# One side's products of the inverse joins as 32 of 32x64 instead of 64 of 32x32

## The chip, the cores and the metric

The kernel runs on one core of a Trainium2 chip. The metric is the device time of one execution in microseconds; the time of a version is the median of several runs. The engines are named as in the profile: PE is TensorE (PEld its weight loads), DVE is VectorE, ACT is ScalarE, POOL is GpSimd and SP is SyncE.

## The reference, cut to what matters

One layer of a hybrid encoder on 528 tokens (16 meta tokens and 512 of the input), model width 1024. Beside an attention branch and an MLP it has a recurrent branch with 8 heads of width 64, a delta rule that goes token by token:

```python
def step(S, inp):
    rt, wt, kt, vt, at, bt = inp
    sa = jnp.einsum('bhij,bhj->bhi', S, at)
    S = S * wt[:, :, None, :] + sa[..., None] * bt[:, :, None, :] + vt[..., None] * kt[:, :, None, :]
    yt = jnp.einsum('bhij,bhj->bhi', S, rt)
    return S, yt

_, y = lax.scan(step, s0, xs)
```

The two branches are gated, projected and added to the residual; then comes an MLP with a squared ReLU of inner width 4096. Everything is float32.

## The kernel before

The recurrence is done in 9 chunks of 64 tokens. Within a chunk the delta rule needs the inverse of a unit triangular 64x64 matrix, one for each head and chunk. The function `inverse` (line 960) makes them for a group of four heads at a time; there are two groups, so it runs twice, g = 0 and g = 1. Four heads lie as two pairs (`pr_`), two heads of a pair on the two halves of the 128 partitions.

An inverse is made from small blocks upwards. DVE inverts the 16x16 diagonal blocks by 15 steps of substitution (lines 985 and 986), all blocks at once. Then come two joins on PE. In the first, 16x16 blocks are joined to 32x32 ones; each of the four quadrants of 32 partitions (`qs[0]` to `qs[3]`) holds one such block. In the second (lines 1033 and 1040), the even and the odd quadrant of a head are joined to the 64x64 inverse. The first join has three groups of products for the 16 cells (8 chunks by 2 pairs):

- line 1011: the lower blocks times `Dn`, the inverses of the 16x16 blocks; DVE masks the result into `W2` (line 1012; the trace calls this tile AX, whose memory it has);
- line 1017: the inverse times `W2`, which line 1021 adds to `Dn`. `Dn` is then read by line 1033, and only its quadrants 0 and 2;
- line 1020: `W2` times the inverse, which line 1025 adds to `Tt`, the placed inverse. `Tt` is read by lines 1040 and 1099.

`Tt` has 64 columns for each cell: in an even quadrant the 32x32 inverse stands in columns 0 to 31 and zeros in columns 32 to 63, in an odd quadrant the other way round (line 993).

The products are in float32, so that PE makes each of them in two passes: 64 products are 128 MATMUL instructions in the trace, and 128 LDWEIGHTS (weight load) instructions on PEld beside them.

All of the first half of the kernel is emitted by a planner, the classes `Clock` and `Turns` (lines 63 and 150). The recurrent branch, the attention, its features and the projections of the input (`projections`, line 553, its matmuls in line 579) are generators that emit some instructions and then give a time from which they can go on. The planner emits the one with the best rank that is ready at its own modelled PE time, and fills with projections (rank 8) otherwise. That order is PE's program order, fixed at build time. The modelled cost of a matmul (lines 121 to 131) hangs on its columns and its tile, with 0.1 us when the tile's form changes; thus an edit of a few matmuls can move the order of those behind it. PE executes strictly in that order. DVE and ACT follow the order too, within the scheduler's priorities.

Behind an inverse stands the chain of its group (`chain`, line 1044): for each of 9 chunks line 1093 on PE, `Rs` on DVE, line 1099 on PE, `uv` on DVE, line 1121 on PE, the next state on DVE. Projections and attention are laid between them. In the second half of the kernel (from line 1222), output projections and MLP, PE goes through matmul after matmul.

Of the kernel before, what the change touches and what calls it, by code (L numbers as in the profile page):

```python
# [187 lines left out]
def kernel(ctx, tc, ht, x, win, par, cst, gain, lora, wout, wo, wup, wdn, out, dbg=None):  # L188
    nc = tc.nc
    dbg = dbg or {}  # L190
    mm = nc.tensor.matmul
# [94 lines left out]
    with ExitStack() as st:  # L286
# [213 lines left out]
        Tt = rp.tile([128, NCH, 2, 64], F32, name="Tt")  # L500
# [4 lines left out]
        hss = [slice(0, 64), slice(64, 128)]  # L505
# [454 lines left out]
        def inverse(g, Bms, late):  # L960
# [35 lines left out]
            Dn, W2 = (AX_[i][:, :64 * LIVE].rearrange("p (a b) -> p a b", b=32) for i in (1, 0))  # L996
            V.tensor_copy(Dn, At[:, :, 2:n2].rearrange("p t n -> p n t"))
            qs = [slice(32 * q, 32 * q + 32) for q in range(4)]
            cells = [(2 * c + pr_ - 2, pr_, c) for c in range(1, NCH) for pr_ in range(2)]

            def half(q):
                return qs[q % 2]

            def bank(name):
                return psm(name).rearrange("p (a b) -> p a b", b=32)

            yield lambda: max(ck.ready(Dn), banks(1))
            p1 = bank("pw")
# [4 lines left out]
            yield lambda: max(ck.ready(W2, Tt), banks(2))  # L1013
            p1, p2 = bank("pw"), bank("pw")
            for n, pr_, c in cells:
                for q in range(4):
                    mm(p1[qs[q], n, :], Tt[qs[q], c, pr_, half(q)], W2[qs[q], n, :], start=True, stop=True)
            for n, pr_, c in cells:
                for q in range(4):
                    mm(p2[qs[q], n, :], W2[qs[q], n, :], Tt[qs[q], c, pr_, half(q)], start=True, stop=True)  # L1020
# [9 lines left out]
            p1 = bank("pw")  # L1030
# [6 lines left out]
            p1 = bank("pw2")  # L1037
# [133 lines left out]
        def recurrent():  # L1171
# [4 lines left out]
            for g in range(2):  # L1176
                prs = pairs[2 * g:2 * g + 2]
                for j, q in enumerate(prs):
# [19 lines left out]
                    if j == 0 and g > 0:  # L1198
                        yield normalised[0][1]
                    yield from q.bonus()  # L1200
                yield from inverse(g, [q.Bm for q in prs], (lambda: pairs[2].ask_keys(inverted[0])) if g == 0 else lambda: None)
                inverted[g].done = True
                turns.add(0, chain(g, prs))
# [30 lines left out]
    with ExitStack() as st:  # L1234
# [5 lines left out]
        for m in range(KB):  # L1240
            w = ahead.pop() if ahead else load_w(wout[m])
            pp = []
            for br in range(2):
# [4 lines left out]
                n = 0  # L1248
# [59 lines left out]
        for i in range(4):  # L1308
            po = ppo()
            n = 0  # L1310
# [289 lines left out]
```

## Time and profile before

| | |
|---|---|
| time, median of 3 runs | 837.0 us (835.97 to 838.46) |
| time of the profiled execution | 836.0 us |
| its span in the profile | 834.2 us |
| PE busy | 810.9 us, 97% |
| DVE busy | 605.0 us, 73% |
| ACT busy | 452.7 us, 54% |
| mean granted clock of PE | 0.994 |
| first inverse, lines 1011 to 1040 | 112.9 to 131.8 us |
| second inverse, lines 1011 to 1040 | 285.4 to 305.9 us |

A row of the timeline reads: start in us from the span's start, duration in us, engine, line, operation, tile written and tiles read, tile of the array (rows*columns), operand shape, how many instructions were put together, and in brackets the engine's idle time before them with what ended it. "issue" there means that nothing in the profile ended it. Matmuls are pipelined, so the rows of consecutive groups overlap. A row of the windows has the busy time and, in brackets, the number of instructions of each engine in that stretch, then the granted clock of PE (1.00 is full speed) and the DMA load. A row of the waits has the total in us, the number of times and the longest. The rows of the DMA queues have packets, MB, and the time of the packets as a share of 16 engines' time.

### The profile page before, as it was taken

The page shows a single profiled execution, that of the slowest core. Times are in us where ns is not written, and L with a number is a line of the kernel's source. Part 1 is how long each engine was busy: PE and PEld are TensorE (multiplying, and loading weights), DVE is VectorE, ACT ScalarE, POOL GpSimd, SP SyncE. Part 2 cuts the span into 40 slices and gives each one's busy share as a digit, 9 for nine tenths or more (in the row PEclk, how much of TensorE's full clock was granted, in tenths as well). Part 3 has the DMA queues.
Part 4 walks back from the last instruction along what each step waited for, and adds up shares of the span by engine and source line. Part 5 has one row for each costly group of instructions (what it writes and reads, how often), then busy time and mean ns, then how long its engine had stood idle before and what let it go on. Part 6 is the DMA issues. An engine that isn't in the chain of part 4 may idle for free.

```text
span 834.2 us, 15768 instructions
## 1 busy us (share of the span) xinstructions
PE 810.9 (97%) x6014; PEld 666.4 (80%) x6014; DVE 605.0 (73%) x1197; ACT 452.7 (54%) x941; POOL 123.1 (15%) x123
## 2 busy tenths in 40 slices
PE   8989989999999899999999999999999999999998
PEld 6979877777868777677878889888888888888886
DVE  6797975596878836676356744975698679867988
ACT  7767537766666347764456623665345434543452
POOL 1031000010001000000022002100650074007400
PEclk9999999999999989999999999999999999999999
DMA  7231221221121402123587603632743274336532
GB/s 239 69 100 55 74 70 55 65 83 59 51 90 52 128 28 79 43 85 102 171 274 223 214 14 122 182 102 59 244 155 98 90 226 153 87 113 203 157 109 75
DMA packets 51484, 95.90 MB, mean 115 GB/s; under 512 B 5832, under 2 KB 7240, under 8 KB 51408
## 3 DMA queue, kind: packets, MB, share of 16 engines
q1 hardware_dynamic: 47680, 86.37, 32.8%
q0 software_dynamic: 1280, 4.20, 1.7%
q10 hardware_dynamic: 2448, 4.33, 1.5%
q8 instruction: 47, 0.77, 0.4%
q14 instruction: 29, 0.24, 0.1%
HBM read 88.56 MB, written 6.31 MB: 114 GB/s over the span
## 4 chain that ended last, share of the span: by engine, by line
PE 85%; DVE 7%; ACT 3%; issue 2%; DMA 2%; SPq 0%; DVEq 0%; ACTq 0%
PE pj L579 22%; PE po L1341 21%; PE po L1468 12%; PE pd L1468 5%; PE po L1251 4%; PE po L1313 3%; PE pj L394 1%; PE pd L1282 1%; PE po L1282 1%; PE psc L740 1%; PE py L794 1%; PE psr L948 1%; PE pssq L674 1%; DVE wlo L549 1%; PE ppt L777 1%
## 5 line engine op out<-in xcount | busy, mean ns | idle before, releaser
L579 PE MATMUL pj<-uhi,whi 128*128 128x264 f32 (+1 forms) x480 | 166.8, 347 | 0.0
L579 PE MATMUL pj<-uhi,wlo 128*128 128x264 f32 (+1 forms) x480 | 154.5, 322 | 2.5 <-DVE wlo L549 2.5
L579 PE MATMUL pj<-ulo,whi 128*128 128x264 f32 (+1 forms) x480 | 154.5, 322 | 0.0
L240 DVE TENSOR_TENSOR wlo<-wraw,whi 128x512 fp32r<-128x512 f32 x84 | 82.5, 993 | 33.5 <-ACT whi L240 33.5
L579 PEld LDWEIGHTS pj<-uhi,whi 128*128 128x128 f32 x480 | 91.0, 190 | 13.7 <-issue 5.3
L579 PEld LDWEIGHTS pj<-uhi,wlo 128*128 128x128 f32 x480 | 90.9, 189 | 9.8 <-DVE wlo L549 2.9
L579 PEld LDWEIGHTS pj<-ulo,whi 128*128 128x128 f32 x480 | 91.2, 190 | 6.6 <-issue 1.9
L1341 PE MATMUL po<-zlo,whi 128*128 128x512 f32 (+1 forms) x248 | 94.8, 382 | 0.0
L1341 PE MATMUL po<-zhi,whi 128*128 128x512 f32 (+1 forms) x248 | 94.8, 382 | 0.0
L1341 PE MATMUL po<-zhi,wlo 128*128 128x512 f32 (+1 forms) x248 | 94.8, 382 | 0.0
L240 ACT CAST whi<-wraw 128x512 fp32r<-128x512 f32 x84 | 51.2, 616 | 51.4 <-PE po L1341 17.0
L548 ACT CAST whi<-wraw 128x512 fp32r<-128x512 f32 x78 | 47.8, 617 | 43.4 <-PE pj L579 40.7
L549 DVE TENSOR_TENSOR wlo<-wraw,whi 128x512 fp32r<-128x512 f32 x78 | 53.8, 695 | 17.6 <-ACT whi L548 17.2
L1390 POOL TENSOR_TENSOR t<-traw 128x512 f32<-128x512 f32 x24 | 38.6, 1626 | 173.1 <-DMA traw<-in_wdn 120.9
L274 ACT CAST whi<-t 128x512 fp32r<-128x512 f32 x64 | 39.9, 623 | 44.5 <-DVE wlo L274 27.2
L1468 PE MATMUL po<-wlo,fhi 128*128 128x512 f32 (+1 forms) x164 | 63.4, 387 | 0.1
L1468 PE MATMUL po<-whi,flo 128*128 128x512 f32 (+1 forms) x164 | 62.8, 384 | 0.0
L1468 PE MATMUL po<-whi,fhi 128*128 128x512 f32 (+1 forms) x164 | 62.3, 384 | 0.0
L274 DVE TENSOR_TENSOR wlo<-t,whi 128x512 fp32r<-128x512 f32 x64 | 43.5, 689 | 24.3 <-ACT whi L274 24.0
L1357 ACT CAST fhi<-R 128x768 fp32r<-128x768 f32 (+1 forms) x32 | 30.2, 944 | 48.3 <-DVE R L1364 24.9
L1341 PEld LDWEIGHTS po<-zhi,wlo 128*128 128x128 f32 x248 | 46.6, 188 | 9.1
L1341 PEld LDWEIGHTS po<-zlo,whi 128*128 128x128 f32 x248 | 46.6, 188 | 9.1
(330 smaller groups left out, 1701.8 us busy)
## 6 DMA issues: line engine op xcount, KB each, us to landing
wraw<-in_win SPq DMA_DIRECT2D x84, 256.0 KB, 2.6
wraw<-in_wup SPq DMA_DIRECT2D x60, 256.0 KB, 3.1
wraw<-in_wdn SPq DMA_DIRECT2D x48, 256.0 KB, 2.7
traw<-in_wdn SPq DMA_DIRECT2D x48, 256.0 KB, 3.5
gd<-gt ACTq DMA_DIRECT2D x16, 256.0 KB, 2.2
wraw<-in_wout SPq DMA_DIRECT2D x16, 256.0 KB, 3.8
gl<-gd SPq DMA_DIRECT2D x16, 256.0 KB, 3.5
traw<-in_wdn POOLq DMA_DIRECT2D x16, 256.0 KB, 3.1
```

The source lines that it names most:

```text
L240: casts.append((A.copy(hi, raw), low.tensor_tensor(lo, raw, hi.bitcast(F32), ALU.subtract)))
L274: return A.copy(hi, x), V.tensor_tensor(lo, x, hi.bitcast(F32), ALU.subtract)
L548: after(A.copy(hi, raw), last["ACT"])
L549: after(V.tensor_tensor(lo, raw, hi.bitcast(F32), ALU.subtract), last["DVE"])
L579: mm(po, a, b[:, k, a0:a1], start=n == 0, stop=n == 23)
L1251: mm(po, a, ys[k][:, b, :], start=n == 0, stop=n == 11)
L1282: mm(pd[i], a[:, k, 128 * i:128 * i + 128], b, start=k == 0 and n == 0, stop=k == 7 and n == 2)
L1313: mm(po, a[:, k, 128 * i:128 * i + 128], b[:, k, :], start=n == 0, stop=n == 23)
L1341: mm(po[:, t0:t1], a, b[:, k, t0:t1], start=n == 0, stop=n == 23)
L1357: A.copy(fhi[:, j, a:b], R[:, a:b])
L1390: eng.tensor_tensor(t, sums[c, pair] if c in (T1, T2) else c, d, ALU.add)
L1468: mm(x[i][:, cols], a[:, k, left, 128 * rows:128 * rows + 128], c[:, cols], start=start and k == 0 and n == 0, stop=stop and k == n_pairs ...
```

## The change

```diff
             for n, pr_, c in cells:
-                for q in range(4):
-                    mm(p1[qs[q], n, :], Tt[qs[q], c, pr_, half(q)], W2[qs[q], n, :], start=True, stop=True)
+                for e, hs in enumerate(hss):
+                    mm(p1[hs, n, :], Tt[qs[2 * e], c, pr_, :], W2[qs[2 * e], n, :], start=True, stop=True)
```

For each cell line 1017 now makes two products in place of four. Each takes an even quadrant's rows of `Tt` with all 64 columns as weights and the same quadrant of `W2` as the moving operand, 32 columns, and writes 64 partitions: an even quadrant gets what it got, the odd one beside it gets zeros, since there `Tt` has its zeros. The update of the odd quadrants of `Dn` is left out with that; no later line reads them. Line 1020 and all else stay as written.

The planner's order changes with it. PE in the first inverse, as a difference; the name behind the arrow's first comma is the weights (`Tt`), the one before it the moving operand (AX is `W2`):

```order
 L579 MATMUL pj<-ulo,whi 128x512
 L579 MATMUL pj<-uhi,wlo 128x512
-L1017 MATMUL pw<-AX_1271,Tt 32x32 x64
+L1017 MATMUL pw<-AX_1271,Tt 64x32 x32
 L1020 MATMUL pw<-Tt,AX_1271 32x32 x64
 L579 MATMUL pj<-uhi,whi 128x512
```

Only line 1017's group has changed there: 32 products, 64 MATMUL and 64 LDWEIGHTS instructions in place of 128 and 128. Up to the second inverse PE has no other row in a new place.

PE in the second inverse, as a difference (pj are the projections):

```order
-L1017 MATMUL pw<-AX_3662,Tt 32x32 x64
-L1020 MATMUL pw<-Tt,AX_3662 32x32 x64
+L1017 MATMUL pw<-AX_3630,Tt 64x32 x32
+L1020 MATMUL pw<-Tt,AX_3630 32x32 x64
+L579 MATMUL pj<-uhi,whi 128x512
+L579 MATMUL pj<-ulo,whi 128x512
+L579 MATMUL pj<-uhi,wlo 128x512
 L579 MATMUL pj<-uhi,whi 128x512
 L579 MATMUL pj<-ulo,whi 128x512
```

Three projection matmuls have moved ahead of the attention's scores (line 740) that follow, and line 1033 stands after nine projections and these scores, where it stood after twelve. Line 1040 follows nine projections behind line 1033, as before; the three that are left over come behind line 1040.

PE at the second chain's first step, before (pch and Rs are the chain's tiles, ppt the attention's transposes):

```order
L1093 MATMUL pch<-uv,L_3467 64x64
L775 MATMUL ppt<-cs,pm_450 48x128
L777 MATMUL ppt<-cs,pe_4121 128x128 x2
L777 MATMUL ppt<-cs,pe_4129 128x128 x2
L1099 MATMUL pch<-Rs,Tt 64x64 x4
```

and now:

```order
L1093 MATMUL pch<-uv,L_3435 64x64
L579 MATMUL pj<-uhi,whi 128x264
L579 MATMUL pj<-ulo,whi 128x264
L579 MATMUL pj<-uhi,wlo 128x264
L579 MATMUL pj<-uhi,whi 128x264
L579 MATMUL pj<-ulo,whi 128x264
L579 MATMUL pj<-uhi,wlo 128x264
L1099 MATMUL pch<-Rs,Tt 64x64 x4
```

Between lines 1093 and 1099 six short projections stand where the transposes stood. Such shifts go on through the first steps of the second chain; from its fifth chunk on the order is that of before again.

## The prediction

> **What bounds the kernel now.** I read the page first.
>
> ```profile
> span 834.2 us, 15768 instructions
> PE 810.9 (97%) x6014; PEld 666.4 (80%) x6014; DVE 605.0 (73%) x1197; ACT 452.7 (54%) x941; POOL 123.1 (15%) x123
> q8 instruction: 47, 0.77, 0.4%
> PE 85%; DVE 7%; ACT 3%; issue 2%; DMA 2%; SPq 0%; DVEq 0%; ACTq 0%
> ```
>
> PE is busy 97% of the span and is 85% of the chain that ended last. What PE saves or loses reaches the end nearly whole, unless a later wait takes it back. So the next view is what PE waits for, its two longest entries, and those of line 1011 and of the chain:
>
> ```profile
> PE pw L1020 <- issue: 5.8, 2, 3.5
> PE pj L579 <- DVE wlo L549: 2.5, 1, 2.5
> ...
> PE pw L1011 <- DVE AX L997: 1.8, 2, 0.9
> PE pch L1099 <- DVE Rs L1095: 1.7, 3, 0.7
> ```
>
> The largest wait of the whole execution stands in line 1020, right behind the edited products: 5.8 us in two holes, and nothing in the profile ends them. The timeline of PE around the first inverse, then the second:
>
> ```profile
> 117.22 1.26 PE L1017 MATMUL pw<-AX,Tt 32*32 32x32 f32 x126
> ...
> 118.33 1.07 PE L1020 MATMUL pw<-Tt,AX 32*32 32x32 f32 x102
> 121.72 0.46 PE L1020 MATMUL pw<-Tt,AX 32*32 32x32 f32 x24 [2.32 <-issue]
> 122.10 0.80 PE L579 MATMUL pj<-uhi,whi 128*128 128x512 f32 x1
> ...
> 126.53 1.20 PE L1033 MATMUL pw<-AX,Bm 32*32 32x32 f32 x64
> 127.66 0.73 PE L740 MATMUL psc<-ka,qa 64*128 64x272 f32 x4
> 128.32 0.50 PE L579 MATMUL pj<-uhi,whi 128*128 128x512 f32 x1
> ...
> 130.59 1.20 PE L1040 MATMUL pw<-Tt,W 32*32 32x32 f32 x64
> ```
>
> ```profile
> 286.55 0.50 PE L579 MATMUL pj<-uhi,whi 128*128 128x512 f32 x1
> ...
> 288.79 1.26 PE L1017 MATMUL pw<-AX,Tt 32*32 32x32 f32 x126
> ...
> 293.88 1.50 PE L1020 MATMUL pw<-Tt,AX 32*32 32x32 f32 x95 [3.52 <-issue]
> ...
> 300.94 1.20 PE L1033 MATMUL pw<-AX,Bm 32*32 32x32 f32 x64
> ```
>
> Line 1020 stops in its middle, where no instruction has anything to wait for: 102 of its passes are through in the first case, about 33 in the second. The windows show that each hole costs twice, since the granted clock falls to half behind it (0.50 in the column behind POOL):
>
> ```profile
> 118.49:121.90 3.41, 1.09 (x125) 0.97 (x116) 1.49 (x3) 0.54 (x2) 0.00 (x0) 1.00 0.04 12
> 121.90:125.31 3.41, 3.41 (x32) 2.67 (x21) 1.41 (x2) 0.00 (x0) 0.00 (x0) 0.50 0.02 5
> ...
> 292.57:295.98 3.41, 2.10 (x97) 1.94 (x97) 0.54 (x1) 0.00 (x0) 0.00 (x0) 0.50 0.02 5
> 295.98:299.39 3.41, 3.41 (x10) 1.86 (x9) 2.06 (x8) 0.31 (x1) 0.00 (x0) 0.50 0.00 0
> ```
>
> **Where the holes come from.** My reading is that PE has run out of program. The page's q8 is a queue of 47 packets, kind "instruction", 0.77 MB. PE and PEld have 12,028 instructions; 0.77 MB over these is 64 bytes each, and 12,028 / 47 is 256 in a packet. So q8 carries PE's program, 256 instructions at a time. The windows from the start to each hole count what had been issued:
>
> ```profile
> 0.00:120.50 120.50, 112.81 (x1240) 97.98 (x1241) 97.54 (x211) 78.66 (x163) 15.71 (x37) 1.00 0.33 105
> 0.00:292.50 292.50, 276.39 (x3017) 230.19 (x3018) 224.94 (x553) 183.64 (x423) 24.68 (x51) 0.99 0.27 85
> ```
>
> That is 2,481 and 6,035, and their difference, 3,554, is 14 packets of 256 less 30 (semaphore events of PE's queue are not in these counts). So both holes stand at a packet's edge. And packets come in just there. In the DMA queues asked by window, 118.9 to 120.3 has the first of these rows, 120.4 to 121.7 none; 286.6 to 287.9 has the second, 287.9 to 291.5 none, 291.5 to 292.5 the third:
>
> ```profile
> q8 instruction: 1, 0.02, 5.7%
> ```
>
> ```profile
> q8 instruction: 1, 0.02, 5.3%
> ```
>
> ```profile
> q8 instruction: 1, 0.02, 5.5%
> ```
>
> In both cases PE goes on soon after a packet that began late. A packet spans 17.7 us on average (834.2 / 47); lines 1017 and 1020 with 512 instructions burn two in 2.3 us. How fast can packets follow each other? PE passed the edge before the first hole at instruction 2,481 - 256, which is 203 instructions into line 1017, at 118.1; the next packet could be used at 121.72, 3.6 us later. In the second, from 289.05 (61 into line 1017) to 293.88, 4.8 us. So 256 instructions need 3.6 to 4.8 us of supply, and the holes are that less the 1.1 us in which PE used them.
>
> **The change part by part.**
>
> *The 32 products themselves.* They are 64 passes instead of 128. Before, four quadrants ran side by side, 128 passes in 1.1 us. Lines 1033 and 1040 are 64 passes of the same 32 moving columns on two quadrants, and take 1.20 as rows, 1.1 to the next group: half the products, the same time, since each quadrant still makes 32 passes. The new line 1017 also has two row groups, so it gains nothing on PE itself. It may lose, because its weights have 64 columns. The nearest rows for that:
>
> ```profile
> L1033 PEld LDWEIGHTS pw<-AX,Bm x128: 101/108/109, 126.5 to 301.9; 32*32 32x32 f32 x128
> ```
>
> ```profile
> L1099 PEld LDWEIGHTS pch<-Rs,Tt x144: 129/134/136, 139.1 to 375.5; 64*64 64x64 f32 x144
> ```
>
> 32 more weight columns make a load 26 to 28 ns longer. A pass in a quadrant now takes 1.1 us / 32 = 34 ns; if the load hides behind the pass, line 1017 stays at 1.1 us; if it sets the pace, a pass is about 34 + 26 = 60 ns, and line 1017 takes 1.9 us. I take 1.85 (+0.75 each time), since the load is now twice as wide as the operand that would have to hide it; both ends stay for the range. A gain is excluded: per row group the passes are the same 32.
>
> *Two changes of the array's form* in place of none, between the new tile (32x64) and line 1020's: bounded by nothing below and a matmul's whole length above (about 0.2 us, each L1033 pass); I take 0.1 per inverse.
>
> *128 instructions less in each inverse.* This is the term that counts, because the edges of the packets stay where they are in the count and the program slides past them. First inverse: the edge of the hole was instruction 459 from line 1017's start (256 + 203). Lines 1017 and 1020 are now 128 + 256 = 384 long, so it lies 75 behind them: past the twelve projections (24 instructions), 51 into line 1033. From the edge before it (75 into line 1020) PE now takes 181 / 256 of 1.1 us, 0.1, the twelve projections, and 51 / 128 of line 1033. Nine projections took 130.59 - 128.32 = 2.27 us at full clock, twelve are 3.03. Sum 0.78 + 0.1 + 3.03 + 0.45 = 4.4 us against a supply of 3.6 to 4.8: a hole of 0 to 0.4.
>
> Second inverse: its edge was 317 behind line 1017's start, which itself now comes 128 earlier: 445, or 61 past line 1020's end, 35 into line 1033 (9 projections and the scores are 26). From the edge before, 61 into line 1020: 0.84 + 0.1 + 2.27 + 0.66 (scores, 128.32 - 127.66) + 0.31 = 4.2 us, a hole of 0 to 0.6. And the edge before that now lies at the end of line 1011: 0.2 + 2.24 (286.55 to 288.79) + 1.1 to 1.85 + 0.26 = 3.8 to 4.5 us, a hole of 0 to 1.0. I take 0.3 for each inverse. Holes this short are below the 2.3 and 3.5 us that cost clock, so the half-speed stretches go too.
>
> On this the Trainium skill speaks against me: "Runtime: NRT & Kernel Launch", section "Instruction fetch mechanics", has the program fetched in blocks of 256 instructions while the engine executes, and calls that cost mostly hidden, because dispatch is slower than the fills. The block agrees with 12,028 / 47; that dispatch is slower does not hold in line 1017's row. By its rule the holes are something else and stay, and the sum below would be rival 2's.
>
> *What the waits behind it do.* Line 1033 needs line 1025 on DVE:
>
> ```profile
> 122.22 1.41 DVE L1025 SCALAR_TENSOR_TENSOR Tt<-pw,even,Tt 128x512 f32<-128x512 f32 x2 [2.00 <-PE pw L1020]
> ```
>
> 1.41 us, under the nine to twelve projections (2.27 to 3.03 us) between lines 1020 and 1033; without them PE would wait these 1.4. DVE now has line 1021 ahead of one softmax step in each inverse, so that this step waits for line 1017's end; it sits idle there anyway (2.00 above). The moved rows of the second inverse and the chain are the same work in another place, taken at nothing; they hide behind projections, and the price if they don't is rival 4.
>
> **The sum**, against the profiled execution. First inverse, from line 1017's start to line 1033's: 126.53 - 117.22 = 9.31 us before; 1.85 + 0.1 + 1.1 + 3.03 = 6.08 now: 3.2 us less. Second: 300.94 - 288.79 = 12.15 before; the same pieces (twelve projections, the scores) 6.08 + 0.66 = 6.74 now: 5.4 us less. Together 8.6, less 0.6 for short holes: 8.0 us. The profiled execution took 836.0 us, so 828.0; it was 1.0 below the median of 837.0, and the forecast for the median is 829.0. With weights hidden and no hole left the gain is 10.7 (about 826.5); with the short holes at their long end it is 8.6 - 2.0 = 6.6 (830.5).
>
> **The rivals.**
>
> 1. *Part of it comes back.* Either the lead of the first inverse is eaten before the second, where DVE's steps (lines 985 to 997) decide when line 1011 can start, and only 5.4 - 0.3 = 5.1 us stay (832); or the short holes come at their long end, 2.0 us, with one half-speed window of 3.41 us, worth 1.7, left: 8.6 - 3.7 = 4.9 us, also 832. For it: line 1011 waited for DVE before (1.8 us in two). Against: behind the first hole DVE sat idle, so it moves forward with PE. Chance 0.25.
>
> 2. *The holes are no code loading* and come again behind line 1017 at full length, with the half clock. Then only the weight loads tell: 0 to 2 x 0.75 us more, 837.0 to 838.5. The packet edges speak against. Chance 0.09. The page of the skill named above stands on this side.
>
> 3. *The diff does nothing*, because line 1017 is no shorter in time: 837.0, as in 2 and counted there. The order shows 32 for 64, so the instructions do go.
>
> 4. *Slower: the second chain's new order.* With lines 1093, 1099 and 1121 elsewhere among the projections, PE reaches a step before DVE has its operand and stands, strictly in order. Before, the longest such wait was 0.7 us (line 1099 in the waits). If each of the 9 chunks waited 1.2 us more, that is 10.8 against the 8.0 gained: 839.8. It decides from 0.9 us in each chunk. Against it: six projections still stand between lines 1093 and 1099. Chance 0.06.
>
> **How the numbers follow.** The forecast has 0.60, rival 1 0.25, rivals 2 and 3 0.09, rival 4 0.06. A measurement here tells about 0.3% (2.5 us) from no change. The forecast and rival 1 are faster by more: 0.85, of which I give 0.01 to "same" for rival 1 falling short: 0.84; same 0.10; slower 0.06. For the range, the forecast's own ends are 826.5 and 830.5; half a microsecond of scatter below, and rival 1 with the runs' scatter of 1.5 above, give 826.0 to 833.5.
>
> **What would show it.** Right: no "issue" wait of over 1 us in line 1020, PEclk at full speed in both inverses, line 1017 with 64 passes in 1.1 to 1.9 us, line 1033 about 3 and then 8 us earlier than before. Short holes, if any, in line 1033. Wrong: the holes still in line 1020; or gone while PE's waits for DVE grow by as much.

## The result and the profile after

The changed kernel takes 828.63 us, the median of 4 runs (827.75 to 828.87). The kernel before, on the same chip, took 837.15 (835.97 to 838.46, 4 runs). The ratio is 0.9896, with a 95% interval of 0.9879 to 0.9913. The forecast was 829.0 in a range of 826.0 to 833.5. The profiled execution took 828.85 us, where that of before took 836.0; their spans are 7.1 us apart. The last experiment below had one run of 996.73 us at a mean granted clock of 0.751, which its figure leaves out.

The page of the changed kernel, its lines on the span, the engines, the program queue and the chain:

```profile
span 827.1 us, 15510 instructions
PE 809.1 (98%) x5886; PEld 666.0 (81%) x5886; DVE 603.5 (73%) x1197; ACT 452.7 (55%) x941; POOL 123.4 (15%) x123
q8 instruction: 46, 0.75, 0.4%
PE 84%; DVE 9%; ACT 4%; issue 2%; DMA 1%; DVEq 0%; ACTq 0%; SPq 0%
```

PE has 128 MATMUL and 128 LDWEIGHTS instructions fewer, and q8 brings one packet fewer: 11,772 / 46 is again 256 in a packet. PE's busy time fell by only 1.8 us. Its idle time, the span less the busy time, fell by 5.3 us, from 23.3 to 18.0. The longest wait of PE after the change, and two that the prediction speaks of:

```profile
PE pj L579 <- DVE wlo L549: 2.5, 1, 2.5
...
PE pw L1011 <- DVE AX L997: 1.8, 2, 0.9
...
PE pch L1099 <- DVE Rs L1095: 1.4, 2, 0.8
```

Line 1020, which led this list with 5.8 us, is no longer in it, and line 1033 has not come in. The wait of line 1099 is 1.4 us, where it was 1.7. The timeline of PE around the first inverse:

```profile
118.67 2.05 PE L1017 MATMUL pw<-AX,Tt 32*64 32x32 f32 x64
...
120.65 1.29 PE L1020 MATMUL pw<-Tt,AX 32*32 32x32 f32 x128
121.87 0.50 PE L579 MATMUL pj<-uhi,whi 128*128 128x512 f32 x1
...
124.81 1.20 PE L1033 MATMUL pw<-AX,Bm 32*32 32x32 f32 x64
```

and around the second:

```profile
287.04 2.05 PE L1017 MATMUL pw<-AX,Tt 32*64 32x32 f32 x64
...
289.02 1.29 PE L1020 MATMUL pw<-Tt,AX 32*32 32x32 f32 x128
290.24 0.50 PE L579 MATMUL pj<-uhi,whi 128*128 128x512 f32 x1
...
293.38 1.20 PE L1033 MATMUL pw<-AX,Bm 32*32 32x32 f32 x64
...
298.25 0.50 PE L579 MATMUL pj<-uhi,whi 128*128 128x512 f32 x1
```

Line 1020 now runs through, 128 passes in one row with no bracket. The windows over the same stretches (line 1017's start to line 1033's) show PE busy throughout at full clock, 1.00 in the column behind POOL, where there were half-speed windows before:

```profile
118.67:124.81 6.14, 6.14 (x205) 5.29 (x204) 3.66 (x11) 2.43 (x9) 0.00 (x0) 1.00 0.15 47
287.04:293.38 6.34, 6.34 (x207) 4.95 (x206) 4.52 (x17) 1.52 (x6) 0.00 (x0) 1.00 0.27 90
```

The edited products themselves got slower. Line 1017 takes 118.67 to 120.65, that is 1.98 us, where it took 1.1. Its view by source line shows why (the times are shortest, median and longest in ns):

```profile
L1017 PEld LDWEIGHTS pw<-AX,Tt x128: 128/133/133, 118.7 to 288.8; 32*64 32x64 f32 x128
L1017 PE MATMUL pw<-AX,Tt x128: 217/218/239, 118.7 to 288.9; 32*64 32x32 f32 x128
```

A weight load of 64 columns takes 133 ns, against 108 for 32 columns in line 1033. The two row groups each make 32 passes in 1.98 us, the step to line 1020 included; that is 62 ns a pass, where it was 34.

One stretch differs by accident, ahead of the inverses. In each profiled execution PE waits 2.5 to 2.8 us for DVE (the first row of the waits above), here from 49.0 to 51.5 us, and in this one the clock fell to half behind it for 3.41 us. The windows for the same stretch, before and after the change:

```profile
51.50:57.00 5.50, 5.50 (x66) 4.04 (x67) 5.47 (x10) 1.77 (x5) 2.37 (x3) 1.00 0.56 181
```

```profile
51.50:57.00 5.50, 5.50 (x39) 4.07 (x40) 4.89 (x9) 0.97 (x4) 2.37 (x3) 0.69 0.62 186
```

Half of 3.41 us is 1.7. So line 1011 starts at 114.4 after the change and at 112.9 before, though PE's program is the same up to there. From line 1011's start to the end it is 827.1 - 114.4 = 712.7 us after, and 834.2 - 112.9 = 721.3 before: 8.6 us less. The experiments below are compared by this stretch too, since what is placed or lost ahead of it is not in it.

### The profile page after: what moved, and what is told of

Same layout as the page of the kernel before. It is cut to its first block, busy times and chain, and to the rows that moved or that the text cites. A ratio compares the mean times of both kernels' runs of the same rounds, so it can differ in the third digit from the quotient of the medians.

```text
span 827.1 us, 15510 instructions
## 1 busy us (share of the span) xinstructions
PE 809.1 (98%) x5886; PEld 666.0 (81%) x5886; DVE 603.5 (73%) x1197; ACT 452.7 (55%) x941; POOL 123.4 (15%) x123
## 4 chain that ended last, share of the span: by engine, by line
PE 84%; DVE 9%; ACT 4%; issue 2%; DMA 1%; DVEq 0%; ACTq 0%; SPq 0%
PE po L1341 21%; PE pj L579 21%; PE po L1468 12%; PE pd L1468 5%; PE po L1251 4%; PE po L1313 3%; PE pj L394 1%; PE po L1282 1%; PE pd L1282 1%; PE psr L948 1%; PE psc L740 1%; PE py L794 1%; DVE wlo L549 1%; PE pssq L674 1%; PE ppt L777 1%
## 5 line engine op out<-in xcount | busy, mean ns | idle before, releaser
L240 DVE TENSOR_TENSOR wlo<-wraw,whi 128x512 fp32r<-128x512 f32 x84 | 77.6, 934 | 35.2 <-ACT whi L240 35.1
L549 DVE TENSOR_TENSOR wlo<-wraw,whi 128x512 fp32r<-128x512 f32 x78 | 53.7, 695 | 18.7 <-ACT whi L548 18.3
L1341 PEld LDWEIGHTS po<-zhi,whi 128*128 128x128 f32 x248 | 46.6, 188 | 9.0
```

The costliest lines, as they stand in the source:

```text
L240: casts.append((A.copy(hi, raw), low.tensor_tensor(lo, raw, hi.bitcast(F32), ALU.subtract)))
L549: after(V.tensor_tensor(lo, raw, hi.bitcast(F32), ALU.subtract), last["DVE"])
L1341: mm(po[:, t0:t1], a, b[:, k, t0:t1], start=n == 0, stop=n == 23)
```

## The experiments

**Theory.** PE runs out of program at a packet's edge when two packets are used up faster than one arrives. The change wins because 128 instructions fewer in each inverse put the edges where PE uses its program slowly; the products themselves lose. **Rival A:** the holes belong to lines 1017 and 1020, to their tiles or their waits, and the new form of line 1017 removes them. **Rival B** (by the rule of the Trainium skill, "Runtime: NRT & Kernel Launch", section "Instruction fetch mechanics", that the loading of program is mostly hidden): the holes are no code loading at all, and would not follow a count of instructions.

Three kinds of edit tell them apart: unused products added 100 us ahead, which shift the edges and touch nothing else; a pause between lines 1017 and 1020, which thins the burst and leaves all products; and the products of the even quadrants alone in the old form, which save the same number of instructions as the change. The line numbers of the rows are shifted where an edit adds lines above: with 18 or 32 unused products, lines 579, 1017 and 1020 of the kernel are 581, 1019 and 1022, with the pause line 1020 is 1022, and with two adds for line 1021 line 1033 is 1034. The kernel before was run again beside the experiments, 13 times each: 837.41 us beside the first four, 836.37 beside the last four. The ratios are to these.

### 72 unused instructions ahead, in the changed kernel

```diff
                     mm(warm[:, :128], ones, ones, start=True, stop=True)
+                for i in range(18):
+                    mm(warm[:32, :32], ones[:32, :32], ones[:32, :32], start=True, stop=True)
```

> The changed kernel with 18 extra 32x32 products (72 instructions of PE) in the warm-up at the start, where PE stands waiting anyway; the rest of PE's order is the same. Theory (PE's program comes in packets of 256, and a packet that PE uses up in less than 3.6 to 4.8 us leaves a hole): the edges of the packets move 72 instructions earlier in the program, so that nearly a whole packet is line 1020's burst (1.2 to 1.3 us). A hole of 2.3 to 3.6 us comes back in both inverses, right behind the end of line 1020 in the first and some ten instructions before its end in the second, each with half clock behind it; 8 to 10 us slower than the changed kernel, 834 to 840 us, although the inverses are untouched. Rival (fewer products in line 1017 are what helped, or the holes belonged to the tile of line 1017): no hole, 828 to 830 us.

Measured: 834.99 us (830.95 to 841.98, 10 runs), ratio to before 0.9984 (0.9955 to 1.0013); the profiled execution took 833.74. That is 6.4 us above the changed kernel, and the two intervals of the ratio do not meet. The timeline of PE in the two inverses:

```profile
123.57 0.40 PE L581 MATMUL pj<-uhi,whi 128*128 128x512 f32 x1
124.23 0.39 PE L581 MATMUL pj<-ulo,whi 128*128 128x512 f32 x1 [0.27 <-issue]
...
290.42 1.25 PE L1022 MATMUL pw<-Tt,AX 32*32 32x32 f32 x125
...
293.49 0.31 PE L1022 MATMUL pw<-Tt,AX 32*32 32x32 f32 x3 [1.81 <-issue]
```

The windows from the start into each hole:

```profile
0.00:123.90 123.90, 117.26 (x1240) 101.70 (x1241) 98.70 (x213) 78.74 (x163) 15.68 (x37) 0.99 0.33 102
0.00:293.00 293.00, 279.66 (x3017) 233.25 (x3018) 225.22 (x553) 183.75 (x423) 24.66 (x51) 0.99 0.27 85
```

1240 + 1241 is 2,481 and 3017 + 3018 is 6,035: the holes have come back at the very instruction numbers they had before the change. In the first inverse that number now falls among the projections behind line 1020, and not into its products. This is against both rivals. The sizes were missed: 0.3 and 1.8 us where 2.3 to 3.6 was expected, and 6.4 us of loss where 8 to 10 was. In the first hole 256 instructions lie between 121.59 and 124.23, so this packet was there after 2.6 us, not after 3.6 or more. That the slow line 1017 (2 us for 128 instructions) gives the loading a head start is a reading; the last experiment speaks for it. From within the second hole on the clock was at half for 6.83 us:

```profile
291.93:298.76 6.83, 5.27 (x15) 3.33 (x15) 2.24 (x6) 0.04 (x1) 0.00 (x0) 0.50 0.01 2
```

From line 1011 on it is 832.0 - 115.3 = 716.7 us, 4.0 more than in the changed kernel, and line 1011 starts 0.9 us later. That is the 4.9 us between the two profiled executions; the other 1.5 of the medians' 6.4 us lie in runs whose traces were not kept.

### 128 unused instructions ahead, in the kernel before

```diff
                     mm(warm[:, :128], ones, ones, start=True, stop=True)
+                for i in range(32):
+                    mm(warm[:32, :32], ones[:32, :32], ones[:32, :32], start=True, stop=True)
```

> The kernel before with 32 extra 32x32 products (128 instructions of PE) in the warm-up at the start; the rest of PE's order is the same. Theory: the holes move with the packets' edges, 128 instructions earlier in the program: in the first inverse line 1020 stops after some 38 passes where it stopped after 102 to 104, in the second the edge moves out of line 1020 into line 1017 (a short hole of 0.4 to 1.5 us there) and the next edge brings the full hole after some 94 passes of line 1020, where it was after 33. Time about as before, 836 to 839 us. Rival (the holes belong to the program's place, not to the count): after 102 and 33 passes as before.

Measured: 838.24 us, a single run. The timeline of PE and the windows up to the two long holes:

```profile
121.33 0.54 PE L1022 MATMUL pw<-Tt,AX 32*32 32x32 f32 x38
124.17 1.12 PE L1022 MATMUL pw<-Tt,AX 32*32 32x32 f32 x88 [2.31 <-issue]
...
293.16 0.42 PE L1019 MATMUL pw<-AX,Tt 32*32 32x32 f32 x28 [0.32 <-issue]
...
297.17 0.45 PE L1022 MATMUL pw<-Tt,AX 32*32 32x32 f32 x31 [2.70 <-issue]
```

```profile
0.00:123.50 123.50, 115.41 (x1240) 100.08 (x1241) 97.63 (x211) 78.66 (x163) 15.72 (x37) 0.99 0.33 102
0.00:296.50 296.50, 280.29 (x3145) 233.50 (x3146) 225.12 (x553) 183.67 (x423) 24.69 (x51) 0.99 0.27 84
```

The first hole stands at 2,481 again, now 64 passes earlier in line 1020 (38 are through, not 102). In the second inverse there are two. The short one, in line 1017 (1019 here), stands at 6,035 again (3017 + 3018 up to 293.1 us), and the long one at 6,291, which is 6,035 + 256, one packet on. So the holes follow the count of PE's instructions and not a place in these lines; with the products unchanged in form, they moved when only the count did.

### A pause between lines 1017 and 1020, in the kernel before

```diff
                     mm(p1[qs[q], n, :], Tt[qs[q], c, pr_, half(q)], W2[qs[q], n, :], start=True, stop=True)
+            begun = ck.pe
+            yield lambda: begun + 3.0
             for n, pr_, c in cells:
```

The planner fills the 3 us with projections and scores. All 64 products stay.

> The kernel before with all 64 products of line 1017, but with a pause of 3 us of the planner's time between lines 1017 and 1020, which it fills with projections and scores; later rows move with it. Theory: the number of small products is not what counts but that 512 instructions are asked for in 2.3 us. With 9 to 12 projections and scores between them (2.5 to 3 us) the packets come nearly in time: no hole over 1 us in the first inverse, one or two of 0.5 to 1.9 us in the second, clock mostly full; 827 to 832 us. Rival (the change helped because it has fewer or other products): holes and half clock as before, 835 us or more.

Measured: 827.41 us (826.86 to 829.01, 4 runs), ratio 0.9887 (0.9871 to 0.9904). The timeline of PE:

```profile
118.96 1.30 PE L1017 MATMUL pw<-AX,Tt 32*32 32x32 f32 x128
...
123.34 1.29 PE L1022 MATMUL pw<-Tt,AX 32*32 32x32 f32 x128
...
288.26 1.01 PE L1017 MATMUL pw<-AX,Tt 32*32 32x32 f32 x96 [0.56 <-issue]
...
292.08 1.29 PE L1022 MATMUL pw<-Tt,AX 32*32 32x32 f32 x128
```

As fast as the change, with the full number of products in the old form; one hole of 0.56 us is left, within line 1017. It stands at 5,779 (2889 + 2890 up to 288.1 us), which is 6,035 - 256: again a packet's edge. Rival A is out: the form need not change for the long holes to go. Here it was enough that the 512 instructions are not used in one piece.

### The even quadrants alone in the old form

```diff
-                for e, hs in enumerate(hss):
-                    mm(p1[hs, n, :], Tt[qs[2 * e], c, pr_, :], W2[qs[2 * e], n, :], start=True, stop=True)
+                for q in (0, 2):
+                    mm(p1[qs[q], n, :], Tt[qs[q], c, pr_, half(q)], W2[qs[q], n, :], start=True, stop=True)
...
-            V.tensor_tensor(Dn, Dn, p1, ALU.add)
+            for q in (0, 2):
+                V.tensor_tensor(Dn[qs[q]], Dn[qs[q]], p1[qs[q]], ALU.add)
```

The same 128 instructions as the change, with weights of 32 columns. The odd quadrants of `Dn` are not updated, as in the change.

> The changed kernel with line 1017 as 32 products of 32x32, the even quadrants alone, in place of 32 of 32x64; line 1021 adds the even quadrants alone, as two instructions on DVE. As many instructions on PE as in the changed kernel, but weights of 32 columns and no change of the array's form before line 1020. Theory: the changed kernel's line 1017 takes 2.0 us because its pass is paced by the load of 64 columns; with 32 columns it takes 1.1, and 0.9 us go from each inverse; a hole of up to 1.0 us may come in line 1020 of the second inverse, whose packet is now used up sooner. 826.0 to 828.0 us. Rival (the two row groups, not the weights' width, set the pace): 2.0 us as in the changed kernel, 828 to 829.5 us.

Measured: 826.89 us (826.28 to 828.48, 4 runs), ratio 0.9878 (0.9864 to 0.9893). No wait named "issue" stands in PE's waits. The timeline of PE in the first inverse, then line 1020 in the second, and line 1017's view:

```profile
118.62 1.16 PE L1017 MATMUL pw<-AX,Tt 32*32 32x32 f32 x61
...
119.65 1.27 PE L1020 MATMUL pw<-Tt,AX 32*32 32x32 f32 x126
...
124.47 1.20 PE L1034 MATMUL pw<-AX,Bm 32*32 32x32 f32 x64
...
287.07 1.61 PE L1020 MATMUL pw<-Tt,AX 32*32 32x32 f32 x126
```

```profile
L1017 PEld LDWEIGHTS pw<-AX,Tt x128: 101/108/108, 118.6 to 287.0; 32*32 32x32 f32 x128
```

Line 1017 takes 119.65 - 118.62 = 1.0 us instead of 1.98, and the stretch from line 1011 on is 824.9 - 114.3 = 710.6 us, 2.1 less than with the change, close to twice 1.0. So the wider weights cost about 1 us in each inverse. Line 1020 takes 1.61 us in the second inverse where it takes 1.27 in the first: 0.33 us pass between two of its instructions at number 5,779, a packet's edge once more. The view of the waits does not show it, since the matmuls' rows overlap; the short hole that was expected there has come. By the medians this version is 1.7 us below the change, but their intervals overlap.

### 256 unused instructions ahead, in the changed kernel

```diff
+                for i in range(64):
+                    qd = slice(32 * (i % 4), 32 * (i % 4) + 32)
+                    mm(warm[qd, :32], ones[qd, :32], ones[qd, :32], start=True, stop=True)
```

> The changed kernel with 64 extra 32x32 products on four quadrants in the warm-up: 256 instructions of PE, one whole packet, so that the edges of the packets fall on the same instructions of the inverses as in the changed kernel; the rest of PE's order is the same. Theory: no hole in either inverse, and from line 1011's start to the end the same time as in the changed kernel (827.1 - 114.3 = 712.8 us, give or take 1); the extra products may delay the start by up to 3 us: 828 to 832 us. Rival (extra work in the warm-up is what slowed the kernel with 72 extra instructions): more extra work, so more loss, 835 us or more, and 717 us or more from line 1011 on.

Measured: 829.78 us (828.09 to 831.52, 4 runs), ratio 0.992 (0.9895 to 0.9944), and no "issue" wait in PE's waits. From line 1011 on it is 827.0 - 114.3 = 712.7 us, as in the changed kernel. So in the profiled executions 72 instructions give back half the gain of this stretch and 256 give back none. That is what packets of 256 predict; the rival, by which more unused work costs more, falls.

### Even quadrants and pause together, and the same with the 72 instructions

The kernel with the even quadrants alone, and between lines 1017 and 1020:

```diff
+            begun = ck.pe
+            yield lambda: begun + 3.0
```

> The even quadrants alone as 32 products of 32x32 (as in the fourth run) and the pause of 3 us of the planner's time between lines 1017 and 1020 (as in the third). Theory: neither inverse has a hole over 0.5 us; the run with the even quadrants alone had none either, so there is little left to gain: 825.5 to 828.0 us. Rival (the pause alone brings something beyond the holes): under 825.5 us.

Measured: 826.21 us (825.08 to 827.46, 4 runs), ratio 0.9882 (0.986 to 0.9904); no "issue" wait, though line 1020 (1022 here) has 0.28 us between two instructions in the second inverse, at number 6,032, three short of an edge. It is level with the version without the pause, which had only 0.33 us left to save. The pause moves the chain too: line 1099 waits 3.1 us for `Rs` where it waits 0.6 without it, and the clock is 0.57 in the window from 142 to 146 us. With the 18 unused products of the first experiment added:

> The same kernel (even quadrants alone, pause between lines 1017 and 1020) with the 18 extra 32x32 products (72 instructions) in the warm-up. Theory: with the pause no packet is used up in under 2.6 us wherever its edges fall, so that the shift costs at most short holes: within 2 us of the kernel without the extra products, 826 to 829.5 us, single runs within 3 us of each other. Rival (any shift by 72 costs as much as it did the changed kernel): 832 us or more.

Measured: 827.45 us (826.73 to 828.18, 4 runs), ratio 0.9892 (0.9874 to 0.9909). No "issue" wait stands in this profile either. From line 1011 on, it is 825.0 - 115.4 = 709.6 us, against 823.3 - 112.9 = 710.4 without the unused products. The 710.4 hold the slow clock at 142 us, which this kernel's profile lacks: 3.41 us at half clock, 1.7 us of work. Without it the unused products would have cost about 1 us here. With these products, but without the pause:

> The even quadrants alone as 32 products of 32x32, no pause, with the 18 extra 32x32 products (72 instructions) in the warm-up. Theory: the edge lies at line 1020's start, its packet is used up in 1.1 to 1.3 us, and holes of 1 to 3 us come back in line 1020 or right behind it, with half clock behind some: 830 to 838 us, with runs spread over 5 us or more. Rival (what came back in the padded changed kernel hung on its 64-column weights or its change of form): no holes, 826.5 to 829 us.

Measured: 834.34 us (833.67 to 835.92, 9 runs), ratio 0.9973 (0.996 to 0.9986). From line 1011 on, 833.6 - 117.5 = 716.1 us. The timeline of PE and the windows into the two holes:

```profile
125.98 0.39 PE L581 MATMUL pj<-ulo,whi 128*128 128x512 f32 x1 [0.76 <-issue]
...
294.94 0.32 PE L1022 MATMUL pw<-Tt,AX 32*32 32x32 f32 x3 [2.43 <-issue]
```

```profile
0.00:125.70 125.70, 118.79 (x1240) 102.74 (x1241) 98.77 (x213) 78.74 (x163) 15.71 (x37) 0.99 0.32 100
0.00:294.50 294.50, 280.58 (x3017) 233.76 (x3018) 226.34 (x555) 183.76 (x423) 24.68 (x51) 0.99 0.27 84
```

Once more 2,481 and 6,035. The 72 instructions cost 716.1 - 710.6 = 5.5 us from line 1011 on without the pause, and at most about 1 us with it. The wide spread between runs that was expected of this kernel did not come: these nine lie within 2.3 us.

## Why the prediction was right

**The holes are code loading, and the change moves the edges.** Right, and shown. In six kernels (before, the one with 128 unused instructions, the pause, the even quadrants alone, and two with 72 unused instructions) eleven holes could be counted, and each stands at 2,481, 5,779, 6,035 or 6,291; the last three are 256 apart. The packets of q8 in the same traces fit one by one: when PE goes on, 9 of them have come since the start at 2,481, 22 at 5,779, 23 at 6,035 and 24 at 6,291, whatever the kernel, and the newest had ended 1.2 to 1.6 us before. The edges also moved as worked out: in the changed kernel PE takes 4.26 us from instruction 2,225 to 2,481 and 4.40 from 5,779 to 6,035, where 4.4 and 4.2 were forecast, and both end in line 1033 (57 and 41 instructions in, where 51 and 35 were worked out); from 5,523 to 5,779 it is 4.81, where 3.8 to 4.5 was forecast. So rival 2 falls. The rule of the Trainium skill named above did not hold for these bursts: the holes of 0.3 to 3.5 us were not hidden, where PE had used up 256 instructions in 1.1 to 1.3 us before each of the six long ones.

**The sum.** From the start of line 1017 to that of line 1033 the first inverse takes 6.14 us, where 6.08 was forecast, and 3.17 us less than before. Its pieces miss by little and cancel in part: line 1017 1.98 (1.95 with the change of form), line 1020 1.22 (1.1), twelve projections 2.94 (3.03). The second takes 287.04 to 293.38, 6.34, where 6.74 was forecast; but three projections, 0.7 us, have moved behind line 1040. The prediction put twelve projections into that stretch, and the order shows nine there: a slip of one term. With nine, the pieces are 1.98 + 1.22 (line 1020, 289.02 to 290.24) + 2.27 + 0.66 = 6.13. The other 0.2 us is at the borders: within a block the projections follow each other by 0.23 us, its first and its last take 0.33, and here the scores cut the nine into two blocks. To the end of line 1040 (the next group's start) it was 305.82 - 288.79 = 17.03 us and is 298.25 - 287.04 = 11.21; 0.7 us of the difference are the three projections that now come later. So about 5.1 us came from the second inverse, where 5.4 was forecast, and 8.3 from both, where 8.6 was. All told, the stretch from line 1011 on became 8.6 us shorter, so that 0.3 came from elsewhere in it; 8.0 was forecast with short holes, and the median fell by 8.5. That the total meets the 8.6 of the sum so closely is in part luck, since 0.3 too much in the second inverse and 0.3 from elsewhere cancel. The gain at the best end should read 10.3 instead of 10.7: by the prediction's own terms it is 8.6 + 2 x 0.75 + 2 x 0.1.

**Line 1017 and the change of form.** Line 1017 takes 1.98 us, 0.13 above the value taken and 0.08 beyond the upper end, but this holds both terms. The weight loads of the first inverse in the changed kernel tell them apart:

```profile
118.67 1.94 PEld L1017 LDWEIGHTS pw<-AX,Tt 32*64 32x64 f32 x64 [0.36 <-DVE psc L749]
120.65 1.18 PEld L1020 LDWEIGHTS pw<-Tt,AX 32*32 32x32 f32 x128
```

The last of line 1017's loads takes 0.13 us, so it starts 1.81 us after the first, and a pass is 1.81 / 31 = 58 ns, where 60 was worked out. That makes 1.87 us for the 32 passes, where 1.85 was taken. Line 1020's first load starts 0.17 us after line 1017's last, 0.12 more than a pass, and that is the change of form, taken at 0.1. That the wider weights set the pace was right, as the even quadrants in the old form show. The load is 25 ns longer than one of 32 columns, and a pass 24 to 27 ns longer than the 34 and 31 ns of the old form. That it is the load, and not the products' twice as many output rows, rests on these numbers alone.

**Short holes** of 0.3 us per inverse did not come. The supply was taken from two cases, 3.6 and 4.8 us, as if a packet took about that long. It is no fixed time: in the padded changed kernel a packet was there after 2.6 us, behind the slower line 1017, and with the pause PE went through 256 instructions in 3.5 us without a hole. That short holes cost no clock was right: behind holes of up to 0.76 us the clock stayed full, and each hole of 1.8 us or more had half clock with it. With the even quadrants alone and the same 72 instructions, where line 1017 is fast, the two holes were 0.5 and 0.6 us longer (0.76 and 2.43 for 0.27 and 1.81). So what the change costs in line 1017 it partly gives back in cover.

**DVE's line 1025** stayed hidden: line 1033 is not in PE's waits.

**Rival 1** (part comes back between the inverses): from the start of line 1033 in the first to that of line 1017 in the second it was 288.79 - 126.53 = 162.26 us and is 287.04 - 124.81 = 162.23. Nothing came back. Line 1033 came 1.7 and 7.6 us earlier, where about 3 and then 8 were named; the first lacks the 1.45 us by which line 1011 started later. **Rival 4** (the second chain's order) falls too: line 1099 waits less than before. **Rival 3** falls with the instruction counts.

The profiled span fell by 7.1 us only, because of the half-clock stretch behind the wait that ended at 51.5 us. Such a stretch stands behind that wait in the profiles of six of the eight experiments too, and not in that of before, of the 256 unused instructions, and of the even quadrants with the pause. What decides it was not found.

What stays open: when exactly a packet is asked for. At the holes, the time from one packet's edge to the next was 2.6 to 4.8 us, and no run changed the loading alone.

## What to carry to other kernels

Where an engine idles in the middle of a group of small instructions and nothing in the profile ends the wait, count the engine's instructions from the start to the hole and divide by the packets of the instruction queue: if the hole keeps its number when unused instructions are added ahead, the loading of program is the first suspect. Fewer or larger products then help by their count and their place, not by the work that they save, and such a gain can be lost to the next edit (72 instructions 100 us ahead took back 4.0 and 5.5 us). Laying long matmuls between two bursts of small ones removed the long holes at both places of the edges that were tried (827.45 us with the 72 unused instructions, against 834.34 without the pause); in the kernel before, the same pause left a hole of 0.56 us.

## What was not expected of the hardware

- Weights of 64 columns with only 32 moving columns made each pass 58 ns instead of 31 to 34: line 1017 took 1.98 us in the 32x64 form and 1.0 us in the 32x32 form for the same 64 passes. The columns of zeros cost about as much as the products themselves.
- An add on 32 partitions cost DVE what one on 128 does, as the even quadrants' view of line 1022 shows; line 1021's single add for both took 689 ns in the changed kernel:

```profile
L1022 DVE TENSOR_TENSOR AX<-AX,pw x4: 667/676/685, 119.9 to 288.0; 32x512 f32<-32x512 f32 x4
```

- The same wait of about 2.5 us, ahead of the inverses, had 3.41 us of half-speed clock behind it in seven of the ten profiles and none in the other three. That is worth 1.7 us.
